# Normalising rows into a repeated output: gamma by matmul, wide sums, roots by tile

## The chip, the cores and the metric

One core of one Trainium2 chip. The metric is device time in microseconds (us) of one execution; lower is better.

## The reference

```python
x: (8, 512, 2048) float32, gamma: (2048,) float32
x_rep  = np.repeat(x, 2, axis=1)                                  # every row twice
rms    = np.sqrt((x_rep ** 2).mean(axis=-1, keepdims=True) + 1e-6)
out    = x_rep / rms * gamma                                      # (8, 1024, 2048) float32
```

33.6 MB are read and 67.1 MB written.

## The kernel before

The 4096 rows are cut into 8 tiles of 128 partitions by 4 rows. A tile `y` holds 8 rows of a partition: the load fills rows 4 to 7, the result goes to rows 0, 2, 4, 6, and copies fill 1, 3, 5, 7. There are three such buffers, so load 3 has to wait for store 0.

```python
def square(i, k):                      # one row: ScalarE
    nc.scalar.activation(out=sq[:], in_=ys[i][:, K*(R-1)+k, :], func=Act.Square, accum_out=ss[:])
    nc.scalar.activation(out=rms[:], in_=ss[:], func=Act.Sqrt, scale=inv_d, bias=eps_t[:])
def scale(i, k, rms):                  # one row: VectorE
    nc.vector.reciprocal(out=rstd[:], in_=rms[:])
    nc.vector.scalar_tensor_tensor(out=ys[i][:, R*k, :], in0=ys[i][:, K*(R-1)+k, :],
        scalar=rstd[:], in1=gamma_b[:], op0=Alu.mult, op1=Alu.mult)
def compute(i):
    for k in range(K): scale(i, k, square(i, k))
    repeat(i, 0, K//2, nc.scalar.copy)
    repeat(i, K//2, K, nc.vector.tensor_copy)
...
load(0, nc.sync, parts=2)              # gamma: seven pieces on ScalarE's queue, then GpSimd
for c0, c1 in zip(cuts, cuts[1:]):
    nc.scalar.dma_start(out=gamma_b[0:1, c0:c1], in_=gamma[c0:c1].partition_broadcast(1))
nc.gpsimd.partition_broadcast(out_ap=gamma_b[:], in_ap=gamma_b[0:1, :])
load(1, nc.sync); load(2, nc.sync)
loads_after = {2: (3, 4, 5), 4: (6, 7)}
for i in range(ntiles):                # one queue: stores in order, loads between
    compute(i); store(i, 0, K)
    for j in loads_after.get(i, ()): load(j, nc.sync)
```

## Time and profile before

| | before |
|---|---|
| time, median of 6 runs | 239.38 us (239.31 to 239.87) |
| span of the profiled execution | 237.9 us |
| VectorE, ScalarE busy | 41%, 42% |
| the load and store queue, share of 16 DMA engines' span | 98.5% |
| instructions in the trace | 287 |

The prediction's 239.55 is the median of the three runs that were known when it was written. The trace before is of an execution of 239.72 us, a little above its median.

98.5% of 237.9 us is 234.3 us in which an average DMA engine had a packet under way. A packet of 64 KB takes 2.42 us on one engine, which for 16 engines is 434 GB/s.

### The profile page before, as it was taken

How to read it: one execution, taken by the hardware profiler on the slowest of the kernel's cores; microseconds unless marked ns; L12 is line 12 of the kernel's file. 1: busy time of each engine (PE TensorE's matmuls, PEld its weight loads, DVE VectorE, ACT ScalarE, POOL GpSimd, SP SyncE). 2: the span in 40 equal slices, each digit the busy share in tenths (PEclk: the TensorE clock that was granted, in tenths of full speed). 3: DMA queues.
4: the chain of work that ended last, by engine and by line, in shares of the span. 5: the costliest groups of instructions: out<-in, count | busy, mean ns of one | idle time of the engine just before them, and what ended most of it. 6: DMA issues, size and time to landing. Idle time of an engine off the chain costs nothing.

```text
span 237.9 us, 287 instructions
## 1 busy us (share of the span) xinstructions
DVE 96.5 (41%) x73; ACT 101.0 (42%) x106; POOL 2.5 (1%) x5
## 2 busy tenths in 40 slices
DVE  0049999960000000059999960000199990000000
ACT  2697999900000000099999920000599960000000
POOL 0030000000000000000000000000000000000000
DMA  7999998989899998999998999989998989999994
GB/s 265 436 446 441 441 441 353 530 353 496 386 452 430 397 485 353 441 441 441 441 518 364 464 419 430 452 369 430 435 518 364 518 364 485 397 452 430 408 474 176
DMA packets 2464, 100.69 MB, mean 423 GB/s; under 512 B 279, under 2 KB 285, under 8 KB 286
## 3 DMA queue, kind: packets, MB, share of 16 engines
q1 hardware_dynamic: 2448, 100.66, 98.5%
q14 instruction: 2, 0.02, 0.0%
q10 hardware_dynamic: 14, 0.01, 0.0%
HBM read 33.56 MB, written 67.11 MB: 423 GB/s over the span
## 4 chain that ended last, share of the span: by engine, by line
DMA 58%; ACT 12%; DVE 9%; issue 1%; POOLq 1%; ACTq 1%; SPq 0%
DMA y<-in_x_dram 33%; DMA out_dram<-y 21%; ACT sq L64 8%; DVE y L74 7%; DMA gamma_b<-in_gamma_dram 4%; ACT y L81 3%; DVE y L81 2%; ACT rms L68 1%; POOLq L136 1%; ACTq L95 1%; DVE rstd L73 0%; POOLq L96 0%; SPq L56 0%
## 5 line engine op out<-in xcount | busy, mean ns | idle before, releaser
L64 ACT ACTIVATE sq<-y 128x2048 f32<-128x2048 f32 x32 | 59.7, 1865 | 87.8 <-DMA y<-in_x_dram 87.8
L74 DVE SCALAR_TENSOR_TENSOR y<-y,rstd,gamma_b 128x2048 f32<-128x2048 f32 x32 | 75.3, 2352 | 4.1 <-POOL gamma_b L96 3.0
L73 DVE RECIPROCAL rstd<-rms 128x1 f32<-128x1 f32 x32 | 5.0, 158 | 94.6 <-ACT rms L68 94.3
L81 ACT COPY y<-y 128x4096 f32<-128x4096 f32 x8 | 28.7, 3590 | 1.4 <-DVE y L74 1.4
L81 DVE COPY y<-y 128x4096 f32<-128x4096 f32 x8 | 18.3, 2294 | 0.3
L68 ACT ACTIVATE rms<-ss,eps_t 128x1 f32<-128x1 f32 x32 | 9.4, 295 | 1.0
L64 ACT ACTIVATION_READ_ACCUMULATOR sq<-y 128x1 f32 x32 | 6.0, 187 | 0.0
L64 ACT ACT_TABLE_LOAD x1 | 1.3, 1283 | 3.0 <-issue 3.0
L96 POOL PARTITION_BROADCAST gamma_b<-gamma_b x1 | 2.3, 2294 | 12.2 <-DMA y<-in_x_dram 12.2
L68 ACT ACT_TABLE_LOAD x1 | 1.3, 1283 | 0.0
L98 DVE MEMSET eps_t<- 128x1 f32 x1 | 0.1, 59 | 0.8 <-PEq L125 0.8
L125 POOL MEMSET const-uint8-127<- 128x1 uint8 x1 | 0.1, 102 | 0.0
L125 POOL MEMSET const-bfloat16-1.0<- 128x1 bf16 x1 | 0.1, 101 | 0.0
L125 POOL MEMSET const-float32-0.0<- 128x1 f32 x1 | 0.1, 98 | 0.2 <-issue 0.2
L125 POOL MEMSET const-float32-1.0<- 128x1 f32 x1 | 0.1, 98 | 0.0
## 6 DMA issues: line engine op xcount, KB each, us to landing
y<-in_x_dram SPq DMA_DIRECT2D x7, 4096.0 KB, 14.6
y<-in_x_dram SPq DMA_DIRECT2D x2, 2048.0 KB, 7.4
out_dram<-y SPq DMA_DIRECT2D x8, 24.4
gamma_b<-in_gamma_dram ACTq DMA_DIRECT2D x6, 1.0 KB
gamma_b<-in_gamma_dram ACTq DMA_DIRECT2D x1, 2.0 KB
```

The costliest lines, as they stand in the source:

```text
L64: nc.scalar.activation(out=sq[:], in_=ys[i][:, K * (R - 1) + k, :], func=Act.Square, accum_out=ss[:])
L68: nc.scalar.activation(out=rms[:], in_=ss[:], func=Act.Sqrt, scale=inv_d, bias=eps_t[:])
L73: nc.vector.reciprocal(out=rstd[:], in_=rms[:])
L74: nc.vector.scalar_tensor_tensor(out=ys[i][:, R * k, :], in0=ys[i][:, K * (R - 1) + k, :], scalar=rstd[:], in1=gamma_b[:], op0=Alu.mult, o ...
L81: copy(out=y_r[:, k0:k1, 1, :], in_=y_r[:, k0:k1, 0, :])
L95: nc.scalar.dma_start(out=gamma_b[0:1, c0:c1], in_=gamma[c0:c1].partition_broadcast(1))
L96: nc.gpsimd.partition_broadcast(out_ap=gamma_b[:], in_ap=gamma_b[0:1, :])
L98: nc.vector.memset(eps_t, eps)
L125: nc = _bacc.Bacc("TRN2", target_bir_lowering=False, num_devices=1)
L136: with _tile.TileContext(nc) as tc:
```

## The change

Its intent: fewer instructions on each engine, and a bound that stays with the transfers. (The tiles lie in SBUF, the core's main memory; PSUM is the memory into which the matmuls write here.) Cut to its core:

```diff
+    gamma_b = junk.tile([P, D], f32, name="gamma_b")          # in PSUM now
+    nc.scalar.preload_act_table(Act.Sqrt)
+    load(0, 0, H)                                             # all on the sync queue
+    for c0, c1 in zip(cuts[:-2], cuts[1:-1]): gamma_piece(c0, c1)
+    load(0, H, K)
+    gamma_piece(cuts[-2], cuts[-1])
+    for c0 in range(0, D, 512):
+        nc.tensor.matmul(gamma_b[:, c0:c0+512], ones[:], gamma_row[:, c0:c0+512], ...)
-    nc.gpsimd.partition_broadcast(out_ap=gamma_b[:], in_ap=gamma_b[0:1, :])
+    def square(i, k0, k1):       # several rows in one instruction, into the output rows
+        nc.scalar.activation(out=ys[i][:, k0:k1, :], in_=ys[i][:, x_at+k0:x_at+k1, :], func=Act.Square)
+    def reduce(i, k0, k1, ss):
+        nc.vector.tensor_reduce(out=ss[:, k0:k1], in_=ys[i][:, k0:k1, :], op=Alu.add, axis=X)
+    def root(k0, k1, ss):        # GpSimd, one root for a tile
+        nc.gpsimd.tensor_scalar(out=at, in0=at, scalar1=inv_d, scalar2=eps, op0=mult, op1=add)
+        nc.gpsimd.tensor_tensor(out=at, in0=at, in1=power_t[:, k0:k1], op=Alu.pow)
+    def root_quick(k0, k1, ss):  # ScalarE's root, VectorE's reciprocal
...
+    by_rows(0, whole)                                  # row sums, root_quick for two rows
+    two = mixed(sums(1, 1), shared, ahead=(2, 1))      # wide squares, reduce, root
+    mixed(two, shared)
+    by_rows(3, shared)
+    _, _, ss = mixed(sums(4, H), whole, ahead=(5, 0))
+    ... tile 5: ScalarE scales, VectorE multiplies by gamma, GpSimd repeats ...
+    last = mixed(sums(6, 1), by_scalar, ahead=(7, 0))
+    mixed(last, shared)
```

The order of the large loads and stores on the queue stays as it was.

## The prediction

> **What bounds the kernel now.** I read the profile in this order: the page's busy shares and DMA rows, to see what is full; the groups of instructions, for what one operation costs; the timeline of the issuing queue and its waits, to see when each transfer is issued and whether the transfers ever run dry. The page first:
>
> ```profile
> span 237.9 us, 287 instructions
> DVE 96.5 (41%) x73; ACT 101.0 (42%) x106; POOL 2.5 (1%) x5
> DMA  7999998989899998999998999989998989999994
> q1 hardware_dynamic: 2448, 100.66, 98.5%
> HBM read 33.56 MB, written 67.11 MB: 423 GB/s over the span
> ```
>
> No compute engine is busy half of the time, and the DMA digits are 8 or 9 from the second slice to the last but one. The kernel is bound by moving 100.7 MB. What the change can win is what the 1.5% outside "98.5%" holds; what it can lose is any time in which compute hands a finished tile over too late and the queue runs empty. So I need the hand-over times. The groups give the cost of one operation:
>
> ```profile
> L64 ACT ACTIVATE sq<-y 128x2048 f32<-128x2048 f32 x32 | 59.7, 1865 | 87.8 <-DMA y<-in_x_dram 87.8
> L74 DVE SCALAR_TENSOR_TENSOR y<-y,rstd,gamma_b 128x2048 f32<-128x2048 f32 x32 | 75.3, 2352 | 4.1 <-POOL gamma_b L96 3.0
> L81 ACT COPY y<-y 128x4096 f32<-128x4096 f32 x8 | 28.7, 3590 | 1.4 <-DVE y L74 1.4
> L81 DVE COPY y<-y 128x4096 f32<-128x4096 f32 x8 | 18.3, 2294 | 0.3
> ```
>
> And the timeline of the issuing queue (start, length, what; asked by short windows, so that each issue stands alone) gives the schedule:
>
> ```profile
> 27.05 0.35 SPq L56 DMA_DIRECT2D out_dram<-y  x1
> 51.39 0.33 SPq L56 DMA_DIRECT2D out_dram<-y  x1
> 52.84 0.34 SPq L52 DMA_DIRECT2D y<-in_x_dram  x1
> 72.14 0.34 SPq L52 DMA_DIRECT2D y<-in_x_dram  x1
> 91.56 0.33 SPq L52 DMA_DIRECT2D y<-in_x_dram  x1
> 115.86 0.34 SPq L56 DMA_DIRECT2D out_dram<-y  x1
> 140.24 0.34 SPq L52 DMA_DIRECT2D y<-in_x_dram  x1
> 159.63 0.34 SPq L52 DMA_DIRECT2D y<-in_x_dram  x1
> ```
>
> The loads at 52.84, 72.14, 91.56, 140.24 and 159.63 each wait for a store to give its buffer back, so these are the landings of stores 0, 1, 2, 3 and 4. Between the first three lie 19.30 and 19.42 us: an 8.39 MB store takes 19.4 us (434 GB/s) and a 4.19 MB load half, 9.7 us. Counting off that spacing: loads 0 to 2 have landed at 33.4, load 1 at 23.7, load 3 at 101.2 (seen: ScalarE starts on it at 101.18), load 4 at 110.8, load 5 at 120.5, load 6 at 169.3 (seen: 169.34), load 7 at 179.0, stores 5, 6, 7 at 198.4, 217.8 and 237.2. That is the span to within 0.7 us, so nothing is lost between. A transfer must be issued somewhat before the one ahead lands; the first load was issued at 0.72 and the first bytes move in the stretch from 1.5, so I allow 1.3 us, an estimate. The deadlines for stores 0 to 7 are then 32.1, 51.5, 70.8, 119.2, 138.9, 177.7, 197.1 and 216.5. Now they are issued at 27.05, 39.22, 51.39, 115.86, 128.25, 160.08, 184.02 and 196.41: all early, store 3 by only 3.3 us.
>
> **What the Trainium skill says.** "DMA: Bandwidth & Descriptors", Specifications, gives a fabric ceiling of 435 GB/s for a core's 16 engines; the 434 GB/s above agrees, so the stretch between the ends has nothing left to win. "VectorE: DVE Perf Modes", The perf-mode tier table, has fp32 copies at two elements a cycle, reductions and two-tensor operations at one, at 0.96 GHz; here a copy of 4096 took 2.294 us (2.13 and 0.16 fixed), which agrees, and no reduction is in this trace. "GPSIMD Engine Reference", Engine selection, calls one-input elementwise work roughly line-rate and two-input work about twice as slow as VectorE; its section 3.1 measures about 2.6 cycles an element at 1.2 GHz for the latter. No such work is in this trace. "SBUF — State Buffer", Who interferes with whom and the section before it, says VectorE and GpSimd share a port pair that VectorE takes in a two-port mode or with two SBUF inputs; nothing in the trace before shows it.
>
> **The change part by part.** Bytes, tiles, three buffers and the order of large transfers stay. (1) gamma: seven row pieces now ride in the load queue, the last behind the second half of load 0, and four matmuls with ones put gamma into PSUM in place of a GpSimd broadcast of 2.29 us. (2) Tiles 0 and 3 go by rows as before, but with one root for two rows. Tiles 1, 2, 4, 6 square several rows in one ScalarE instruction into the output rows, and VectorE sums them. (3) Roots of tiles 1, 2, 4, 5, 6, 7 become two GpSimd instructions (scale and add, then a power). (4) Tile 5 scales on ScalarE, multiplies by gamma on VectorE and is repeated by GpSimd. Instructions fall from 73 to 28 or so on VectorE and from 106 to under half on ScalarE, but VectorE's work grows by the sums, and it is serial by tile.
>
> Durations, all estimates from the rows above: ScalarE costs 0.136 us plus 0.843 ns per element (from 1.862 at 2048 and 3.590 at 4096), so squares of 4096, 6144, 8192 take 3.6, 5.3, 7.0; a square with its accumulator read takes 2.03 from start to start. VectorE sums take 0.16 plus 1.042 ns an element: 4.4, 6.6, 8.7; a copy of 8192 takes 4.4. The fused scale takes 2.352; I use 2.40 each with gamma in PSUM and gaps, 9.6 for four. A GpSimd root with hand-overs: 1.5, a guess, since the trace has only its memsets of 0.1 us.
>
> Store 0: first half landed at 8.1; the second at 13.0, the last gamma piece just behind, matmul 14.4 (before, the first scale ran at 14.92). Scales and a reciprocal 9.8, copy 4.4: 28.6. Deadline 32.1, spare 3.5. Store 1: load at 23.7, square 29.0, sum 35.6, root 37.1, scales 46.7, copy 49.0; spare 2.5. Store 2: VectorE goes on at 49.0, 6.6 + 1.5 + 9.6 + 2.3 = 20.0, so 69.0; spare 1.8. Store 3: load at 101.2, two sums, root and reciprocal 105.7, two scales 110.5, reciprocal and two scales 115.5, copy 117.8; spare 1.4. Store 4: ScalarE has its squares and sums at 121.8; VectorE from 117.8: sum 122.2, root 123.7, scales 133.3, copy 137.7; spare 1.2. Store 5: sum 146.4, root 147.9, four ScalarE scales 155.4, multiply 164.1; GpSimd's copy of 8192 elements then has until 177.7, 13.6 us. At one element a cycle of 1.2 GHz it needs 7. Store 6: load at 169.3, square 174.6, sum 181.2, root 182.7, scales 192.3, last ScalarE copy 195.9; spare 1.2. Store 7: sum from 192.3 to 201.0, root 202.5, scales 212.1, copy 214.4; spare 2.1.
>
> So every store gets much later than before, and each is still in time. The schedule spends the slack and the path does not move: sum zero.
>
> **The rivals.** First, slow roots. Nothing in the trace prices a GpSimd power, and the kernel keeps ScalarE's root for tiles 0 and 3 under the name "quick", which hints that the power is slow. Stores 2 and 7 have two roots in series behind them, stores 4 and 6 one. With a root of r us, store 2 is late by 2(r - 2.4), store 4 by r - 2.7 more, stores 6 and 7 by about 2(r - 2.55): at 3 us a loss of 2.4 us (242), at 4 us 7.4 us (247). Two per cent is passed near 3.5. Second, GpSimd's copy at the two-input pace of 2.6 cycles an element: 17.7 us, store 5 at 181.8, late by 4.1: about 243.6. VectorE waits for load 6 in that time, so the shared port should not be fought over. Third, a gain: loads 0 to 2 landed at 33.4, of which 29.1 is transfer, 0.7 the first issue and 1.3 latency; at most 2.3 us could come back from a calmer start, since gamma's pieces no longer mix with load 0 in a second queue. That is under 1%. Fourth, the reverse: the small pieces hold one DMA engine up, some tenths. The removed table load and instruction count lie beside transfers and are worth nothing.
>
> **Range and chances.** The sum says no change, 239.55. Small lateness at one or two tight stores is likelier than a gain, so 239.8, range 238.6 to 242.4. Faster by 2% needs 4.8 us, more than the start holds: 0.01. Slower by 2% needs roots over 3.5 us, or the slow copy with something on top: 0.09. Within 2%: 0.90.
>
> **What would show it.** DMA digits of 8 and 9 throughout, and stores issued near 28.6, 49, 69, 118, 138, 165 to 177, 196 and 214. A root's two GpSimd instructions near 1.5 us or not, and GpSimd's copy under 13.6 us or not. If the landings of stores lie over 19.4 us apart where only stores run, a store came late and the prediction is wrong there; VectorE waiting for GpSimd longer than 2.5 us would be the cause.

## The result, and the profile after

The changed kernel took 240.94 us, median of 6 runs (240.41 to 241.29), against 239.38 us (239.31 to 239.87) on the same chip. The ratio is 1.0059, with a 95% interval of 1.0045 to 1.0072. The time is within the predicted range and within 2%, but it is a small, clear loss of about 1.5 us where the prediction's sum was zero.

First the page of the changed kernel, answering to the lines of the page before:

```profile
span 238.6 us, 245 instructions
PE 7.2 (3%) x8; PEld 2.3 (1%) x8; DVE 132.9 (56%) x45; ACT 90.8 (38%) x47; POOL 14.7 (6%) x20
DMA  7999999898989989999989898899999999998984
q1 hardware_dynamic: 2462, 100.67, 98.2%
```

VectorE has taken on 36 us of work in fewer instructions (45 for 73; the prediction had "28 or so"), ScalarE has lost 10 us, and the DMA digits are full as before. 98.2% of 238.6 us is 234.3 us: the engines moved the same bytes in the same time as before. What is longer in this execution is the rest, 4.3 us against 3.6 us.

The groups of the changed kernel (line, engine, operation, shape and count; busy us and mean ns; idle before and who ended it) price what the trace before could not:

```profile
L87 DVE SCALAR_TENSOR_TENSOR y<-y,ss,gamma_b 128x2048 f32<-128x2048 f32 x28 | 64.7, 2345 | 10.5 <-POOL ss L83 7.4
L80 POOL TENSOR_SCALAR ss<-ss 128x4 f32<-128x4 f32 x6 | 1.2, 194 | 168.8 <-DVE ss L74 168.8
L94 POOL COPY y<-y 128x8192 f32<-128x8192 f32 x1 | 7.0, 7011 | 16.6 <-DVE y L194 16.6
L83 POOL TENSOR_TENSOR ss<-ss,power_t 128x4 f32<-128x4 f32 x6 | 6.1, 1009 | 0.5
```

VectorE waited for GpSimd's root 7.4 us in five times, 1.5 us each. And the issues of the stores on the sync queue (start and length, asked by short windows; store 0, issued at 29.24, is left out):

```profile
48.83 0.34 SPq L56 DMA_DIRECT2D out_dram<-y  x1
68.34 0.33 SPq L56 DMA_DIRECT2D out_dram<-y  x1
116.68 0.34 SPq L56 DMA_DIRECT2D out_dram<-y  x1
136.31 0.34 SPq L56 DMA_DIRECT2D out_dram<-y  x1
169.89 0.34 SPq L56 DMA_DIRECT2D out_dram<-y  x1
194.84 0.34 SPq L56 DMA_DIRECT2D out_dram<-y  x1
212.82 0.33 SPq L56 DMA_DIRECT2D out_dram<-y  x1
```

Against the prediction's 28.6, 49.0, 69.0, 117.8, 137.7, 164 to 171, 195.9 and 214.4 none is off by more than 1.6 us. The stores come as late as was worked out, and they are still in time. I followed the trace's packet records along each of the 16 DMA engines: between 10 and 230 us the longest gap on any engine is 0.34 us in the kernel before and 0.05 us in this one. In the changed kernel one single engine ends 1.1 us after the other fifteen, in the kernel before 0.55 us after them. (The records name no engine; they are chained, each packet to the one that ended just before it.)

Part of the rest lies behind the last packet. From its end to the end of the span it takes 1.64 us in the changed kernel and 1.18 in the kernel before. In the closing barrier, where all engines wait for one another, VectorE comes late. The waits of the sync queue there (columns: us in total, times, longest), in the kernel before and in the changed kernel:

```profile
SPq L136 <- PEq L136: 0.6, 2, 0.4
```

```profile
SPq L228 <- PEq L228: 0.9, 2, 0.8
```

The four traces of kernels with GpSimd's roots (this one, again, gamma_act and slow_roots) all take 1.53 to 1.64 us there, the ten others 1.17 to 1.21. Among these ten are the two of quick_roots, an experiment below that differs from the changed kernel in the roots alone. So about 0.35 us of the loss comes with GpSimd's roots; why VectorE then ends late is not shown.

So the late hand-overs that the prediction feared are not in this trace, and yet the kernel is slower. The prediction's sign for a late store, landings over 19.4 us apart where only stores run, does appear: stores 1 and 2 landed at 71.14 and 90.64, stores 3 and 4 at 139.03 and 158.84, 19.50 and 19.81 us apart. Without a stand-still, that sign doesn't tell a late store here. This execution was the fastest of the six (240.41), so it may not hold all of the loss. Three theories went into the experiments: **A**, stores that are queued only two microseconds ahead cost something even without a stand-still; **B**, the start costs, where one DMA engine carries all gamma pieces of the load queue (six of them run back to back from 7.41 to 7.73 us); **C**, packets run long for reasons that no part of the change names. **D** and **E** came later.

### The profile page after: what moved, and what is told of

It is laid out like the page before. It is cut to its first block, busy times and chain, and to the rows that moved or that the text cites. A ratio compares the mean times of both kernels' runs of the same rounds, so it can differ in the third digit from the quotient of the medians. Undisturbed runs are those within 1.5% of the kernel's fastest.

```text
span 238.6 us, 245 instructions
## 1 busy us (share of the span) xinstructions
PE 7.2 (3%) x8; PEld 2.3 (1%) x8; DVE 132.9 (56%) x45; ACT 90.8 (38%) x47; POOL 14.7 (6%) x20
## 3 DMA queue, kind: packets, MB, share of 16 engines
q1 hardware_dynamic: 2462, 100.67, 98.2%
## 5 line engine op out<-in xcount | busy, mean ns | idle before, releaser
L87 DVE SCALAR_TENSOR_TENSOR y<-y,ss,gamma_b 128x2048 f32<-128x2048 f32 x28 | 64.7, 2345 | 10.5 <-POOL ss L83 7.4
L74 DVE TENSOR_REDUCE ss<-y 128x3 f32<-128x6144 f32 (+2 forms) x6 | 41.4, 6903 | 11.1 <-ACT y L69 11.1
L69 ACT ACTIVATE y<-y 128x6144 f32<-128x6144 f32 (+2 forms) x6 | 33.6, 5604 | 26.1 <-DMA y<-in_x_dram 26.1
L63 ACT ACTIVATE sq<-y 128x2048 f32<-128x2048 f32 x13 | 24.4, 1874 | 42.0 <-DMA y<-in_x_dram 41.8
L94 ACT COPY y<-y 128x4096 f32<-128x4096 f32 x6 | 21.6, 3605 | 30.9 <-DVE y L87 30.8
L94 DVE COPY y<-y 128x4096 f32<-128x4096 f32 (+1 forms) x6 | 18.0, 3004 | 0.2
L190 ACT ACTIVATE y<-y,ss 128x2048 f32<-128x2048 f32 x4 | 7.8, 1994 | 18.8 <-POOL ss L83 18.8
L194 DVE TENSOR_TENSOR y<-y,gamma_b 128x8192 f32<-128x8192 f32 x1 | 8.7, 8686 | 9.3 <-ACT y L190 9.3
L94 POOL COPY y<-y 128x8192 f32<-128x8192 f32 x1 | 7.0, 7011 | 16.6 <-DVE y L194 16.6
L127 PE MATMUL gamma_b<-gamma_row,ones 1*128 1x512 f32 x8 | 7.2, 1078 | 8.1 <-DMA gamma_row<-in_gamma_dram 8.1
```

The costliest lines, as they stand in the source:

```text
L63: nc.scalar.activation(out=sq[:], in_=ys[i][:, x_at + k, :], func=Act.Square, accum_out=ss[:, k : k + 1])
L69: nc.scalar.activation(out=ys[i][:, k0:k1, :], in_=ys[i][:, x_at + k0 : x_at + k1, :], func=Act.Square)
L74: nc.vector.tensor_reduce(out=ss[:, k0:k1], in_=ys[i][:, k0:k1, :], op=Alu.add, axis=mybir.AxisListType.X)
L87: nc.vector.scalar_tensor_tensor(out=ys[i][:, R * k, :], in0=ys[i][:, x_at + k, :], scalar=rstd[:, k : k + 1], in1=gamma_b[:], op0=Alu.mul ...
L94: copy(out=y_r[:, k0:k1, 1, :], in_=y_r[:, k0:k1, 0, :])
L127: nc.tensor.matmul(gamma_b[:, c0 : c0 + bank], ones[:], gamma_row[:, c0 : c0 + bank], start=True, stop=True)
```

## The experiments

There were twelve runs, in four batches, each batch beside the kernel before on one chip.

**again**: the changed kernel, unedited.

> The changed kernel once more, unedited, for its size on this chip and a second look. After the first result (240.94 against 239.38, ratio 1.0059) and a trace in which the 16 DMA engines never idle between 10 and 230 us, no theory is settled. All theories: ratio 1.005 to 1.008. If the loss is a late hand-over that only some executions show, this profile should have a store whose issue comes less than 1 us before the transfer ahead of it has ended; if it lies elsewhere, the margins are 1.9 us or more again.

240.84 us median of six, ratio 1.0040 (1.0014 to 1.0066). The six are 239.35, 241.46, 240.76, 240.91, 241.06 and 239.52 us: two are as fast as the kernel before, whose eleven runs of this batch spread from 239.24 to 239.98. The profile is that of the 239.35 us execution. Its store issues differ from the first trace's by 0.3 us at most. So the same program, with the same schedule, can run as fast as the kernel before. The two traces of the changed kernel are 1.07 us apart, and their packets took the same time within 0.1 us; what differs is the end of the last engine: 236.99 us there, 1.1 us after the other fifteen, and 236.03 us here, with them. Between these two executions, then, nearly all of the difference is a single engine that ends late.

**start_only**: the new start, with each tile then computed by rows.

```diff
-    by_rows(0, whole)
-    two = mixed(sums(1, 1), shared, ahead=(2, 1))
-    ... (all tiles as in the change)
+    for i in range(ntiles):
+        by_rows(i, shared)
+        for j in {2: (3, 4, 5), 4: (6, 7)}.get(i, ()): new_tile(); load(j, 0, K)
```

> The changed kernel's start alone (gamma row pieces in the load queue, matmuls with ones into PSUM, one preloaded table, one root for two rows), every tile computed by rows as before, so that stores are ready as early as in the kernel before. Theory A (late stores cost[...]): ratio 0.996 to 1.000, since the first loads landed 0.9 us earlier in the changed kernel. Theory B (the start costs, one DMA engine carries all gamma pieces): ratio 1.005 to 1.007 like the whole change. Theory C (nothing of the program, one DMA engine is disturbed by something else): anything between, not tied to the edit.

240.69 us, ratio 1.0047 (1.0034 to 1.0060); five runs from 240.30 to 241.04. The stores came early again (39.85, 52.60, 130.35 us for stores 1, 2, 4), and the loss is all there. Theory A for those stores doesn't explain this; B seemed to. But store 3 was not early: pairing the rows moved it from 115.86 to 117.59, 1.8 us before the first engine would have run out of packets, where the kernel before has 3.5 and the changed kernel 2.1. For this one store the run doesn't test A.

**quick_roots**: the changed kernel without GpSimd's roots.

```diff
-        root(0, K, ss)
+        root_quick(0, K, ss)          # in mixed(), and for tile 5
```

> The changed kernel with ScalarE's root and VectorE's reciprocal in place of GpSimd's two instructions everywhere. A root then takes about 0.6 us instead of 1.5, so stores 1, 4, 6 come 0.9 us earlier and stores 2 and 7 1.8 us (ScalarE may hold one up while it squares the next tile, as far as 5 us for tile 5). Theory A: part of the loss comes back, ratio 1.002 to 1.005. Theory B: no difference from the changed kernel, 1.005 to 1.008. Theory C: no difference.

239.61 us, ratio 1.0007 (0.9991 to 1.0023). It has the new start, so B alone doesn't explain it either, unless A and B work together.

**late_before**: the kernel before with its stores delayed by an idle sum.

```diff
         repeat(i, 0, K // 2, nc.scalar.copy)
+        if i not in (0, 3):
+            nc.vector.tensor_reduce(out=late[:], in_=y_l[:, 0:15*D//4], op=Alu.add, axis=X)
         repeat(i, K // 2, K, nc.vector.tensor_copy)
```

> The kernel before with an idle VectorE sum of 7680 elements (8.2 us, result not used) ahead of the last copy of tiles 1, 2, 4, 5, 6 and 7. Stores 1, 2, 4, 7 should be issued at about 47.4, 67.7, 136.4 and 212.7 as late as in the changed kernel (48.8, 68.3, 136.3, 212.8), and nothing else changes. Theory A: ratio 1.004 to 1.008. Theory B and C: ratio 0.999 to 1.001.

239.78 us, ratio 1.0010 (0.9996 to 1.0023). The stores came as planned:

```profile
46.86 0.34 SPq L56 DMA_DIRECT2D out_dram<-y  x1
66.96 0.33 SPq L56 DMA_DIRECT2D out_dram<-y  x1
136.60 0.34 SPq L56 DMA_DIRECT2D out_dram<-y  x1
212.70 0.33 SPq L56 DMA_DIRECT2D out_dram<-y  x1
```

The median moved 0.2 us (the plain mean of the seven runs lies 0.24% over that of the kernel before). Delays of 8 to 16 us on a store cost little, as long as it is ahead of the queue's end. Theory A is weakened by this but not felled: only stores 4 and 7 come about as close to the end of the packets ahead as in the changed kernel (2.1 and 3.7 us, against 1.8 and 3.1). Stores 0, 1, 2, 3 and 6 keep 3.4 to 5.6 us, where the changed kernel has 1.7 to 2.2. And four of seven runs lie at 239.5 to 239.8 and the rest reach 241.14, so the spread has grown as in the changed kernel.

**no_compute**: the transfers of the kernel before and no arithmetic; its output is wrong.

```diff
-    compute(i); store(i, 0, K)
+    store(i)                      # rows 0 to 3 of the three buffers set to zero once
```

> Transfers alone: the kernel before's loads and stores in their order on the same queue, with no arithmetic (output wrong on purpose: zeros and unscaled rows). Every store waits only for its load. If the transfers set the end in both kernels, this takes as long as the kernel before: ratio 0.994 to 1.001, DMA share 98% or more, and its own spread shows how much of 1 to 2 us is the transfers' own. If a hand-over by compute costs anything in the kernel before, it is faster than 0.99.

239.16 us, five runs within 0.1 us, ratio 0.9981 (0.9969 to 0.9993). This is the floor for this order of transfers. The kernel before stands 0.2% over it. Nothing done to the computing alone could win 2%, as the prediction had it from the 98.5%.

**gamma_act** and **start_act**: the gamma pieces of the changed kernel, and of start_only, issued from ScalarE's queue again, to test B.

```diff
     load(0, 0, H)
-    for c0, c1 in zip(cuts[:-2], cuts[1:-1]): gamma_piece(c0, c1)     # sync queue
     load(0, H, K)
-    gamma_piece(cuts[-2], cuts[-1])
+    for c0, c1 in zip(cuts, cuts[1:]): gamma_piece(c0, c1)            # ScalarE's queue
```

> The changed kernel with its gamma pieces issued from ScalarE's queue as in the kernel before; the halves of load 0 are again issued back to back. So far late stores alone cost 0.1% (late_before), and the new start with stores on time 0.5% (start_only). Theory B (pieces in the load queue): ratio 0.999 to 1.002. Theory C (packets of some loads or of one DMA engine run long for reasons outside the program): 1.003 to 1.007 as the changed kernel, or anything else without order.

> start_only with its gamma pieces on ScalarE's queue: the new start without its one change to the load queue. Theory B: ratio 0.998 to 1.001, as the kernel before. Theory C: no order; if 1.004 to 1.006 again, the queue of the pieces is not the cause.

244.65 us, ratio 1.0213 (1.0200 to 1.0226), and 242.16 us, ratio 1.0108 (1.0093 to 1.0122). Neither theory foresaw that, and both are misses as tests. The waits of the sync queue in gamma_act, and a stretch of it (columns: stretch, length, busy time of PE, weight loads, VectorE, ScalarE and GpSimd, clock, DMA share, GB/s), show why:

```profile
SPq L51 <- DMA y<-in_x_dram: 6.9, 1, 6.9
```

```profile
7.80:9.00 1.20, 1.03 (x2) 0.54 (x3) 0.00 (x0) 0.97 (x1) 0.00 (x0) 1.00 0.05 14
```

The sync queue waited 6.9 us for a load, and from 7.8 to 9.0 us the DMA share is 0.05: all 16 engines stood still. The second half of load 0 had come to share a semaphore with the first half and was issued only when that had landed. In the changed kernel the same semaphore falls to the last gamma piece, which can afford the wait. The records give 1.4 us in which all stood still (1.3 in start_act), 1.7 us for the average engine. The rest of gamma_act's loss is packet time: 97.3% of 242.9 us is 236.3 us, 2 us more than the changed kernel's 234.3, of which 0.6 us lie before 10 us and 0.9 near 30 us; what made the packets long is not shown.

**quick_roots_2**: quick_roots once more.

> quick_roots unedited once more: at 1.0007 it was the one kernel with the new start and late stores that lost nothing. If that repeats (below 1.002), half a microsecond to a microsecond of earlier stores matters and theory A has something to it in this start; if it comes out at 1.003 or above, a repeat of one program differs by as much as the change, and differences of 0.4% between these kernels can't be laid to an edit.

239.95 us, ratio 1.0021 (1.0001 to 1.0042), from 239.34 to 240.96. So quick_roots also has executions of both kinds, and its first result was on the lucky side. With ratios of 1.0007 and 1.0021 for one program, and 1.0059 and 1.0040 for the changed one, I can't lay a difference of 0.2% to an edit; that the roots' 0.9 us matter for the transfers is not shown. (The 0.35 us of the closing barrier are missing from both its traces.)

**start_act_2**: start_act mended.

```diff
-    nc.scalar.preload_act_table(Act.Sqrt)      # ahead of load 0
     ...
     for c0, c1 in zip(cuts, cuts[1:]): gamma_piece(c0, c1)            # ScalarE's queue
+    nc.scalar.preload_act_table(Act.Sqrt)      # behind the pieces: other semaphores
```

> start_act mended: in start_act and gamma_act the second half of load 0 came to share a semaphore with the first half and waited for it (all DMA engines stood still from 7.8 to 9.1 us), so they tested something else. Here the table load stands behind the pieces on ScalarE's queue, and the second half shares its semaphore with a gamma piece, as in the kernel before. No stand-still at 7.8 us. Theory B (pieces in the load queue): ratio 0.998 to 1.001. Theory C: 1.003 to 1.006 as start_only, or without order.

240.47 us, ratio 1.0036 (1.0021 to 1.0052), with no stand-still at 7.8 us (DMA share 0.97 there). The pieces are back on their own queue and the loss stays.

**pieces_only**: no_compute with the changed kernel's gamma pieces in the load queue.

```diff
     load(0, 0, H)
+    for c0, c1 in zip(cuts[:-2], cuts[1:-1]): gamma_piece(c0, c1)
     load(0, H, K)
+    gamma_piece(cuts[-2], cuts[-1])
```

> no_compute plus the changed kernel's seven gamma pieces in the load queue, and nothing else (output wrong on purpose). no_compute came out at 239.16 us with a spread of 0.1, so it is a fine scale. Theory B: 0.5 to 1.5 us over no_compute, that is a ratio to the kernel before of 1.001 to 1.005. Theory C: within 0.2 us of no_compute, 0.997 to 0.999.

239.29 us (239.24 to 239.44), 0.13 us over no_compute. Together with start_act_2 this fells theory B.

**slow_roots**: the changed kernel with dearer roots, to test the prediction's deadlines.

```diff
+        for _ in range(2):
+            nc.gpsimd.tensor_tensor(out=idle[:, k0:k1], in0=at, in1=power_t[:, k0:k1], op=Alu.pow)
         nc.gpsimd.tensor_tensor(out=at, in0=at, in1=power_t[:, k0:k1], op=Alu.pow)
```

> The changed kernel with two idle powers on GpSimd ahead of each root's own: a root with its hand-overs takes 1.5 + 2.1 = 3.6 us. In the changed kernel's trace stores 1, 2, 4, 6 and 7 come 1.1, 0.9, 0.9, 1.1 and 2.4 us before a DMA engine would run dry (issue time, 1.0 us to the first byte, data end). The prediction's sum with these: store 2 late by 4.2 - 0.9 = 3.3, store 4 by 1.2, store 7 by 1.8 (store 6 by 1.0 of it): 6.3 us more than the changed kernel, 247 us, ratio 1.028 to 1.036, with stand-stills of the DMA engines near 50, 70, 140, 200 and 220 us. If late hand-overs cost nothing like that (the transfers make it up), the ratio stays below 1.015.

245.88 us, ratio 1.0262 (1.0249 to 1.0275). VectorE now waits 3.6 us for a root, store 2 is issued at 72.56, and the queue has run dry before it. First a line of the waits of slow_roots (us in total, times, longest), then a stretch ahead of store 2's first bytes, columns as above:

```profile
DVE y L90 <- POOL ss L86: 17.7, 5, 3.6
```

```profile
71.20:73.20 2.00, 0.00 (x0) 0.00 (x0) 1.28 (x1) 0.00 (x0) 0.00 (x0) 1.00 0.00 0
```

The packet records show stand-stills of all engines before store 1 (0.8 us on average), store 2 (2.2), store 4 (1.0) and store 7 (0.5), 4.5 us in all. The expectation written for this run had 1.0, 2.3, 1.2 and 1.8, 6.3 us, so it was too high at stores 6 and 7, and the ratio fell just below its range. The formulas of the prediction give, at 3.6 us, 2.4 + 0.9 + 2.1 = 5.4 us. The run lost 4.9 us against the changed kernel's 240.94. The sum agrees better than its parts: the formulas have nothing at store 1, which lost 0.8 us, and 2.1 us at stores 6 and 7, which lost 0.6; at stores 2 and 4 (2.4 and 0.9) they fit. The method of deadlines holds: this is what a late store looks like, and the changed kernel's trace has none.

**broadcast**: start_act_2 with gamma in SBUF again. What is left of the change is one root for two rows and one table load.

```diff
-    nc.tensor.matmul(gamma_b[:, c0:c0+bank], ones[:], gamma_row[:, c0:c0+bank], ...)
+    nc.gpsimd.partition_broadcast(out_ap=gamma_b[:], in_ap=gamma_b[0:1, :])
```

> start_act_2 with gamma spread by GpSimd's broadcast into SBUF as in the kernel before, in place of the matmuls into PSUM. What is then left of the change is one root for two rows and one table load. Late stores (0.1%) and the pieces in the load queue (0.05%) have both fallen as the cause of the 0.4 to 0.5% that start_only and start_act_2 lose. Theory D (gamma by matmul in PSUM, read there by VectorE, costs in some way): ratio 0.999 to 1.001. Theory E (the pairing of the rows, or any change of the order of work, shifts when load packets and store packets meet, and packets of some loads run long): 1.002 to 1.005 still.

240.19 us, ratio 1.0034 (1.0020 to 1.0049). Theory D, gamma in PSUM, falls too. Pairing the rows, which moves no store by more than 2 us and takes work off ScalarE, is enough for more than half of the loss. What remains is E, which says little, and A for store 3, which comes 1.9 us ahead here too.

**Where the time is, if not why.** The packet records place most of it. Stretches from 174 to 182 us, where load 7 ends and store 5 begins, in no_compute, the kernel before, the changed kernel, broadcast and start_only, in that order (last two columns DMA share and GB/s; kernels that don't use PE have no columns for it):

```profile
174.00:182.00 8.00, 0.00 (x0) 0.00 (x0) 1.00 1.04 446
```

```profile
174.00:182.00 8.00, 7.86 (x8) 7.94 (x8) 0.00 (x0) 1.00 1.04 446
```

```profile
174.00:182.00 8.00, 0.00 (x0) 0.00 (x0) 6.52 (x2) 4.30 (x3) 1.20 (x2) 1.00 1.00 397
```

```profile
174.00:182.00 8.00, 7.93 (x5) 7.31 (x7) 0.00 (x0) 1.00 1.11 443
```

```profile
174.00:182.00 8.00, 0.00 (x0) 0.00 (x0) 7.93 (x5) 7.31 (x6) 0.00 (x0) 1.00 1.12 434
```

GB/s over share is 429 in the first two, near the usual 434, and 397, 399 and 388 in the others: for 8 us packets took about 9% longer, 0.7 to 0.9 us. The records show it as one packet of nearly every engine that takes 1.4 to 2.5 us instead of 1.2, at the end of load 7. The opposite is seen at 28 to 34 us, where load 2 ends and store 0 begins, in the kernel before and in the changed one:

```profile
28.00:34.00 6.00, 5.93 (x5) 5.94 (x7) 0.00 (x0) 1.00 1.11 410
```

```profile
28.00:34.00 6.00, 0.00 (x0) 0.00 (x0) 6.00 (x2) 3.49 (x4) 0.00 (x0) 1.00 1.08 464
```

Here the kernel before has 369 and the changed kernel 430. So in its two traces the changed kernel won some 0.9 us at the first changeover and lost about 0.6 at the last (and 0.3 near 87 us, by the records). start_only keeps the first loss (1.2 us by the records) and adds the second, and it is slower in every one of its runs: 98.5% of 239.0 us is 235.4 us of packet time, 1.1 us over the 234.3 of the kernel before; broadcast's 98.6% of 238.4 us is 235.1. Second, a single engine or two can end late: in late_before's 241.14 us execution one engine ended 1.4 us after the next.

Nor is a changeover's time fixed by the program. In the two traces of quick_roots, one program whose stores 0 to 2 were issued at the same times to 0.01 us, the stretch from 28 to 34 us reads:

```profile
28.00:34.00 6.00, 0.00 (x0) 0.00 (x0) 6.00 (x2) 1.97 (x3) 0.00 (x0) 1.00 1.06 459
```

```profile
28.00:34.00 6.00, 0.00 (x0) 0.00 (x0) 6.00 (x2) 1.98 (x3) 0.00 (x0) 1.00 1.08 437
```

The quotients are 433 and 405; by the records the average engine lost 0.0 and 0.5 us there, and 0.5 and 0.9 at the changeover near 178 us.

One rival was overlooked. Over all 14 traces the two losses go with how long before the end of the packets ahead a store was issued. At 30 us the five traces with store 0 2.1 to 2.5 us ahead lost 0.0 (four of them) or 0.5 us; the nine with 5.3 us or more lost 0.9 to 1.2. Near 178 us it is the other way round, and with store 3: the ten traces that have it 1.6 to 2.1 us ahead lost 0.25 to 1.0 us, the four with 3.4 or more 0.05 to 0.3. That is an order among traces, not an experiment: no run moved store 0 or store 3 alone, and it doesn't say how store 3 would reach load 7. (At store 0 the lost time itself lengthens the lead, but by 1 us, not by 3.)

Two things stay open. What makes packets run long at a changeover from loads to stores in one execution and not in another: gamma's pieces in either queue, gamma in PSUM or SBUF, GpSimd roots or none don't decide it by themselves, and in no_compute it happens at 30 us with no compute engine busy. And what the slow executions of the changed kernel (241 us) hold, since both of its traces fell on executions under its median.

## Why the prediction was right or wrong

- **Bound by transfers, little to win**: right, and shown by no_compute, 0.2% under the kernel before.
- **The stores' times**: right within 1.6 us. That is no less than the spare of several stores (1.2 to 2.5 us); seven of the eight erred to the early side, which helped. The estimates behind them held: a root with its hand-overs took 1.5 us (a guess in the prediction's own word, so a hit by luck), GpSimd's copy of 8192 elements 7.01 (7 foreseen), the wide sums 6.55 and 8.68, wide squares 5.32 and 7.02 us. The fused scale took 2.345 us, less than the 2.40 assumed. The first scale came at 15.3 instead of 14.4, because the last quarter of gamma needed 2.1 us of weight loads and matmuls after its load, not 1.4; that is why store 0 was issued 0.6 us later than foreseen.
- **The rivals of slow roots and a slow GpSimd copy**: neither came true in the change. slow_roots shows the first one's arithmetic on purpose: 4.9 us measured for a formula's 5.4, with errors at single stores that offset one another.
- **The rival of a calmer start**: partly. ScalarE started on load 3 at 100.25 us instead of 101.18, so 0.9 us was won there, but at the changeover at 30 us; gamma's pieces in the load queue alone win nothing there (pieces_only against no_compute).
- **The sum of zero**: off by 1.5 us, 0.6%. The step that failed is the one that took every transfer as 19.4 or 9.7 us whatever the kernel, so that only stand-stills could cost. The runs show kernels without a stand-still that differ by up to 1.5 us. In the changed kernel's own trace the packets took the same 234.3 us as before (0.9 us won at 30 us, 0.6 and 0.3 lost later); its 0.7 us over the trace before lie in a last engine that ends 0.2 us later and in a closing barrier that takes 0.46 us longer. Neither is a term of the prediction's sum. The prediction leaned to 239.8 for "small lateness at one or two tight stores"; the direction fitted, but no store was late. That the time fell into the range says that the bound was read rightly, not that this loss was foreseen.

## What to carry to other kernels

When the transfers are the bound, turn the schedule into deadlines: read the landings from the issues that wait for buffers, put the new compute times beside them, and see what is spare at each hand-over. Here that reckoning held within 1.6 us for eight stores, and 8 to 16 us of later stores cost 0.1% (0.2% at the top of the interval) where 2 us and more were left. After moving a small transfer to another queue, look which transfer now waits for which: with that mistake start_act lost 0.7% more than start_act_2, and gamma_act about 1.6% more than the changed kernel. And a floor kernel with transfers alone (spread 0.1 us) tells in one run how much there is to win; differences of a few tenths of a per cent between kernels above it need many runs, and even then may belong to no single edit.

## What the Trainium skill lacked or had wrong

- "VectorE: DVE Perf Modes", the errata section, gives a higher fixed cost for a PSUM source than for SBUF (120 against 58 cycles). That row has one source; for two sources of which one is in PSUM no figure stands beside it. With gamma in PSUM and the rows in SBUF the fused scale took 2.345 us, against 2.352 us with both in SBUF: no extra cost for one operand of two.
- "DMA: Bandwidth & Descriptors", the Bandwidth section, has the HBM side (about 358 GB/s) bind transfers between HBM and SBUF, although the same section lists 425 GB/s for one core alone. One core alone held 434 GB/s here for over 200 us, in stores (8.39 MB in 19.4 us) and loads alike, so its sentence on 358 doesn't hold for a core that runs alone. The rate is next to the fabric ceiling of 435 that the page gives; that the fabric bound it no run tests.
- No page that I read has GpSimd's small arithmetic: a scale and add of 128x4 took 0.194 us, a power with 128x4 tensors as base and exponent 1.009 us, and VectorE waited 1.5 us for the pair.
- No page that I read speaks of packets that run long where loads give way to stores: load packets of 1.2 us took up to 2.5 us there, 0.5 to 1.2 us on average per engine, in some executions and not in others.
